# Both heads' scores of a row block issued together, the low key products on 64 rows each, in pairs five to eight

## The chip, the cores and the metric

The kernel runs on one core of a Trainium2 chip. The metric is the device time of one execution in microseconds; the median of three runs of the kernel before is 777.73 us (777.62 to 779.82).

## What is computed

One inference step of a single layer: 512 prompt frames and 64 sample frames (576 columns together) go through a joint projection, two kinds of attention with eight heads of 64 dimensions each, an output projection, an MLP with squared ReLU and a gated embedding. The change touches the scores of the second kind, the sparse attention of the prompt, which picks 128 keys for each query by an indexer's score:

```python
def dsa_attend(q, k, v, iq, ik, iw, q_pos, k_pos, topk):
    logits = jnp.einsum('bqhd,bld->bqhl', iq, ik, preferred_element_type=jnp.float32)
    score = jnp.einsum('bqh,bqhl->bql', iw.astype(jnp.float32), jax.nn.relu(logits))
    ...
    s = jnp.einsum('bqhd,bqkhd->bhqk', q, kg, preferred_element_type=jnp.float32) * HEAD_DIM ** -0.5
    p = jax.nn.softmax(jnp.where(valid[:, None], s, NEG), axis=-1)
    return jnp.einsum('bhqk,bqkhd->bqhd', p.astype(vg.dtype), vg)
```

The kernel doesn't gather keys: it computes all scores of a block and adds a bias that sends the keys not chosen away.

## The kernel before

**Two numbers for one.** A float32 operand is split into a high part that TensorE's F32R type holds and a low remainder, both F32R. A product then takes high by high, low by high and high by low. The projections (`gemm`, line 279) do this with three matmuls of 288 columns for each 128 rows of depth.

**Pairs of heads.** The sixteen heads go in eight pairs, `p` = 0 to 7; 0 to 3 are the forgetting attention, 4 to 7 (pairs five to eight) the sparse one. A pair's queries and keys stand transposed, 64 dimensions of the even head in rows 0 to 63 and of the odd head in rows 64 to 127. For the even head `qE` holds the high part in rows 0 to 63 and the low part in rows 64 to 127, and `kE` the high part in both halves (the second by a DMA, line 737); for the odd head, `qO` and `kO` have the halves the other way round. So one matmul over 128 rows gives high by high and low by high (line 825). The low part of the keys stands in `KL` (buffers `KLP`): rows 0 to 63 for the even head, rows 64 to 127 for the odd one. In pairs one to four the other half of `KL` carries two rows of the forget gate against a row of ones in `Q2`; in pairs five to eight it is zero, and the second matmul (line 827) multiplies 64 rows of keys and 64 rows of zeros.

**Jobs and ticks.** A pair has nine jobs: row blocks `i` = 0 to 3 of 128 queries, each for the even and then the odd head, with (i+1)·128 keys, and one job for the sample frames. Each tick takes one new job, in three micro-steps (`PLAN`, line 917): the first has `addmax` (DVE: scores plus bias, with the row's extreme, line 835) of the job before and `exp` (ACT) of the one before that; the second `ptrans` (transposes on TensorE, tile `T`) of the fourth before; the third `qk` of the new job, `pevac` (copies `T` out of PSUM; DVE in pairs five to eight, line 878) and `pv` (weights times values, line 898). `drive` puts 27 such micro-steps between the 24 pieces of six matmuls of the next pair's projection (`proj`), so TensorE's order is: six projection matmuls, one micro-step, and so on. During pairs five to seven these are the projections of pairs six to eight, during pair eight those of the output projection.

**The ring.** Scores `S`, transposes `T` and the tiles `X` (token-major values in `v_out`, sample outputs in `pv`) take turns in three PSUM banks (tag "R", line 296). A new tile starts once the tile that had its bank has been read: `S` by `addmax`, `T` by `pevac`, `X` by a copy on ACT. Two more facts matter: until pair five DVE also chooses the keys of the sparse attention (lines 642 and 644), and `v_out` of the pair before writes its two `X` tiles in the first two ticks of a pair.

Of the kernel before, what the change touches and what calls it, by code (L numbers as in the profile page):

```python
# [36 lines left out]
def tile_hybrid_step(ctx: ExitStack, tc: tile.TileContext, I, O):  # L37
    nc = tc.nc
    PE, ACT, DVE, POOL, SP = nc.tensor, nc.scalar, nc.vector, nc.gpsimd, nc.sync
# [255 lines left out]
    def psum_1(tag, bufs, dt=F32):  # L295
        return psA.tile([128, 512], dt, name=tag, tag="V" if tag == "V" else "R", bufs=1 if tag == "V" else 3)
# [505 lines left out]
    Q2 = cT = None  # L802
# [9 lines left out]

    def qk(j):
        P = pair[j["p"]]
        ps = psum_1("S", 1)
        if j["s"]:
            g, pp = divmod(j["p"], 4)
            PE.matmul(ps[:, :PAST + NS], QB[j["p"] % 2], KcT[g][:, pp], start=True, stop=True)
            j["S"] = ps[:, :PAST + NS]
        else:  # L820
            i, hh = j["i"], j["hh"]
            n = (i + 1) * 128
            c = slice(i * 128, i * 128 + 128)
            Q, K = P["q" + "EO"[hh]], P["k" + "EO"[hh]]
            PE.matmul(ps[:, :n], Q[:, c], K[:, :n], start=True, stop=False)  # L825
            Q = P["Q2"][:, hh] if j["p"] < 4 else Q
            PE.matmul(ps[:, :n], Q[:, c], P["KL"][:, hh, :n], start=False, stop=True)  # L827
            j["S"] = ps[:, :n]

    def addmax(j):  # L830
        n = j["S"].shape[1]
# [80 lines left out]

    def jobs_of(p):
        out = [dict(p=p, hh=hh, i=i, s=False, close=i % 2 == 1 and hh == 1) for i in range(4) for hh in range(2)]
        return out + [dict(p=p, s=True, close=True)]

    PLAN = (((oevac, 6), (addmax, 1), (exp, 2), (make_bias, 0), (make_bias, -1)),
            ((ptrans, 4), (norm, 2)),
            ((qk, 0), (pevac, 4), (pv, 5)))

    all_jobs = [j for p in range(8) for j in jobs_of(p)]
    tick_no = [0]

# [614 lines left out]
```

## Time and profile before

| | |
|---|---|
| median of three runs | 777.73 us |
| the profiled execution | 777.55 us, of which its span is 775.8 us |
| TensorE busy (matmuls / weight loads) | 765.7 / 749.7 us |
| DVE / ACT / POOL busy | 563.3 / 459.0 / 119.5 us |
| granted TensorE clock | 1.00 throughout |

Rows of the timeline read: start in us from the span's start, duration in us, engine, line of the kernel, operation, output tile and inputs, rows by columns of weights, partitions by elements of the moving operand, count of instructions merged in the row, and in brackets the idle time ahead of it with what ended it. PE are matmuls, PEld are weight loads, which overlap them. A matmul's duration is that from its start to its last result, and successive ones overlap, so what a matmul costs is read from one start to the next.

### The profile page before, as it was taken

Reading aid. Unit: us, or ns where it says so; the run is one execution under the profiler, and the core shown is the slowest. Engines: PE = TensorE matmul, PEld = TensorE weight load, DVE = VectorE, ACT = ScalarE, POOL = GpSimd, SP = SyncE. Lnnn points to the kernel's source line nnn. Section 1 sums busy time; section 2 is a strip of 40 time slices with the busy share of each in tenths; the row PEclk is TensorE's granted clock in tenths of the full one; section 3 lists DMA queues with packets and bytes.
Section 4 is the critical chain, followed back from the end, with each engine's and each line's share of the span. In section 5 each row is a group of like instructions: output and inputs, shape, how many; then the busy total and the mean of one; then the engine's idle time right before and its main releaser. Section 6 shows DMA issues by size and latency. Waiting matters only on the chain.

```text
span 775.8 us, 14798 instructions
## 1 busy us (share of the span) xinstructions
PE 765.7 (99%) x5766; PEld 749.7 (97%) x5766; DVE 563.3 (73%) x1196; ACT 459.0 (59%) x963; POOL 119.5 (15%) x122
## 2 busy tenths in 40 slices
PE   8999999999999999999999999999999999999997
PEld 8989999999999999999999999999999999999997
DVE  7679888897557566899988766767667776657553
ACT  5468777899988644685365443445434455526351
POOL 8117535343421000300000000000000000022100
PEclk9999999999999999999999999999999999999999
DMA  8636334362313225321242322332222314630001
GB/s 304 201 43 148 123 103 117 95 196 85 97 57 104 77 82 185 137 99 56 82 136 87 104 80 60 107 109 82 82 82 82 109 56 124 231 121 29 28 29 68
DMA packets 31126, 81.43 MB, mean 105 GB/s; under 512 B 5072, under 2 KB 10192, under 8 KB 30928
## 3 DMA queue, kind: packets, MB, share of 16 engines
q1 hardware_dynamic: 30768, 80.27, 33.1%
q8 instruction: 45, 0.74, 0.4%
q10 hardware_dynamic: 288, 0.22, 0.1%
q14 instruction: 25, 0.20, 0.1%
HBM read 66.38 MB, written 9.54 MB: 98 GB/s over the span
## 4 chain that ended last, share of the span: by engine, by line
PE 89%; DVE 6%; ACT 2%; issue 1%; DMA 1%; POOL 0%; SPq 0%; DVEq 0%; ACTq 0%
PE g L279 54%; PE m L279 20%; PE n L279 3%; PE V L898 2%; PE T L65 2%; PE S L827 1%; PE S L825 1%; DVE dbias L618 1%; PE m L419 1%; PE m L426 1%; PE S L426 1%; ACT whl L183 1%; PE X L65 1%; DVE whl L187 1%; DVE Y L1203 1%
## 5 line engine op out<-in xcount | busy, mean ns | idle before, releaser
L183 ACT CAST whl<-wraw 128x512 fp32r<-128x512 f32 (+1 forms) x228 | 137.6, 611 | 172.9 <-PE g L279 150.3
L187 DVE TENSOR_TENSOR whl<-wraw,whl 128x512 fp32r<-128x512 f32 (+1 forms) x194 | 132.0, 692 | 69.6 <-ACT whl L183 69.3
L279 PE MATMUL m<-AH,whl 128*128 128x288 f32 x736 | 177.8, 308 | 0.0
L279 PE MATMUL g<-BH,whl 128*128 128x288 f32 (+2 forms) x784 | 162.5, 296 | 0.0
L279 PEld LDWEIGHTS m<-AH,whl 128*128 128x128 f32 x736 | 126.5, 188 | 1.9 <-issue 1.0
L279 PEld LDWEIGHTS g<-BH,whl 128*128 128x128 f32 x784 | 127.7, 188 | 0.3
L279 PE MATMUL g<-BL,whl 128*128 128x288 f32 (+2 forms) x392 | 115.3, 295 | 0.0
L279 PE MATMUL m<-AL,whl 128*128 128x288 f32 x368 | 109.1, 296 | 0.0
L279 PE MATMUL g<-hidO,whl 128*128 128x288 f32 (+2 forms) x768 | 103.8, 295 | 0.0
L279 PE MATMUL g<-hidE,whl 128*128 128x288 f32 (+2 forms) x768 | 103.7, 295 | 0.0
L279 PEld LDWEIGHTS g<-hidO,whl 128*128 128x128 f32 x768 | 102.5, 188 | 0.0
L279 PEld LDWEIGHTS g<-hidE,whl 128*128 128x128 f32 x768 | 102.2, 188 | 0.1
L279 PEld LDWEIGHTS g<-BL,whl 128*128 128x128 f32 x392 | 73.7, 188 | 0.1
L1093 POOL TENSOR_TENSOR ln_s<-Y 128x576 f32<-128x576 f32 (+2 forms) x3 | 4.6, 1519 | 435.2 <-DVE Y L1370 361.9
L279 PE MATMUL g<-s,whl 128*128 128x288 f32 x504 | 71.2, 295 | 0.0
L279 PEld LDWEIGHTS m<-AL,whl 128*128 128x128 f32 x368 | 69.5, 189 | 0.7
L279 PEld LDWEIGHTS g<-s,whl 128*128 128x128 f32 x504 | 68.2, 188 | 0.0
L187 POOL TENSOR_TENSOR whl<-wraw,whl 128x512 fp32r<-128x512 f32 x34 | 44.7, 1314 | 73.6 <-ACT whl L183 49.7
L839 ACT ACTIVATE sP<-sP,st 128x128 f32<-128x128 f32 (+4 forms) x72 | 39.5, 550 | 14.2 <-DVE st L835 13.8
L279 PE MATMUL m<-BH,whl 128*128 128x288 f32 x192 | 43.6, 304 | 0.0
L1346 DVE TENSOR_TENSOR Y<-Y,g 128x576 f32<-128x576 f32 x40 | 29.9, 748 | 14.5 <-PE g L279 14.5
L845 ACT ACTIVATE sP<-sP,st 128x128 f32<-128x128 f32 (+4 forms) x63 | 34.2, 549 | 5.1 <-DVE st L843 4.3
(276 smaller groups left out, 1296.2 us busy)
## 6 DMA issues: line engine op xcount, KB each, us to landing
wraw<-in_w_up_dram SPq DMA_DIRECT2D x32, 512.0 KB, 3.5
wraw<-in_w_down_dram SPq DMA_DIRECT2D x32, 512.0 KB, 3.5
wraw<-in_w_qkv_dram SPq DMA_DIRECT2D x23, 512.0 KB, 3.6
wraw<-in_w_gate_dram SPq DMA_DIRECT2D x8, 512.0 KB, 4.1
wraw<-in_w_o_dram SPq DMA_DIRECT2D x8, 384.0 KB, 3.1
out_vT_dram<-v SPq DMA_DIRECT2D x8, 288.0 KB, 2.1
Y<-in_xT_dram SPq DMA_DIRECT2D x8, 288.0 KB, 4.7
PLD<-PL SPq DMA_DIRECT2D x4, 576.0 KB, 3.0
```

The source lines that it names most:

```text
L65: PE.transpose(out, in_, ident[:n, :n])
L183: ACT.copy(self.hv[h][0], src)
L187: eng.tensor_tensor(lv, src, f(hv), OP.subtract)
L279: PE.matmul(ps, W(w, kw, wc), a[:, ka, cols], start=(first and i == 0), stop=(last and i == n - 1))
L419: PE.matmul(mk[:, h, :HW], w0(part, k), a[:, k, h * HW:(h + 1) * HW], start=(k == 0 and i == 0), stop=(k == 7 and i == 2))
L426: PE.matmul(acc[b][:n[b], :304], a[:, k, b * 128:b * 128 + n[b]], ixw(part, k), start=(k == 0 and i == 0), stop=(k == 7 and i == 2))
L618: DVE.scalar_tensor_tensor(dst[:n, :nk], r[:n, :nk], w, dst[:n, :nk], op0=OP.mult, op1=OP.add)
L825: PE.matmul(ps[:, :n], Q[:, c], K[:, :n], start=True, stop=False)
L839: ACT.activation(j["P"], j["P"], AF.Exp, bias=j["st"][:, 0:1], scale=-1.0, accum_out=j["st"][:, 2:3])
L845: ACT.mul(j["P"], j["P"], j["st"][:, 3:4])
L898: PE.matmul(P["O"][r, (i - 1) * 128 + c.start:(i + 1) * 128], P["vt"][:, kb, r], t[:, hh, kb, c], start=(kb == 0), stop=(kb == i))
L1346: later(0, lambda y=y, m=m: DVE.tensor_tensor(y, y, m[:, :, :HW], OP.add))
```

## The change

In pairs five to eight `qk` of the even head's job issues the scores of both heads of the row block, and `qk` of the odd head's job does nothing. First come the two products over 128 rows, then the two products with the low keys, now over 64 rows each: rows 0 to 63 for the even head, rows 64 to 127 for the odd one, which leaves the zeros out. The two `S` tiles are taken from the ring together. Pairs one to four issue what they issued, and `addmax` and all later stages keep their ticks.

```diff
     def qk(j):
         P = pair[j["p"]]
-        ps = psum_1("S", 1)
         if j["s"]:
+            ps = psum_1("S", 1)
             g, pp = divmod(j["p"], 4)
             PE.matmul(ps[:, :PAST + NS], QB[j["p"] % 2], KcT[g][:, pp], start=True, stop=True)
             j["S"] = ps[:, :PAST + NS]
-        else:
-            i, hh = j["i"], j["hh"]
-            n = (i + 1) * 128
-            c = slice(i * 128, i * 128 + 128)
-            Q, K = P["q" + "EO"[hh]], P["k" + "EO"[hh]]
-            PE.matmul(ps[:, :n], Q[:, c], K[:, :n], start=True, stop=False)
-            Q = P["Q2"][:, hh] if j["p"] < 4 else Q
-            PE.matmul(ps[:, :n], Q[:, c], P["KL"][:, hh, :n], start=False, stop=True)
-            j["S"] = ps[:, :n]
+            return
+        if j["p"] >= 4 and j["hh"]:
+            return
+        i = j["i"]
+        n = (i + 1) * 128
+        c = slice(i * 128, i * 128 + 128)
+        both = [j] if j["p"] < 4 else [j, j["mate"]]
+        for x in both:
+            x["S"] = psum_1("S", 1)[:, :n]
+            PE.matmul(x["S"], P["q" + "EO"[x["hh"]]][:, c], P["k" + "EO"[x["hh"]]][:, :n], start=True, stop=False)
+        for x in both:
+            hh = x["hh"]
+            if j["p"] < 4:
+                PE.matmul(x["S"], P["Q2"][:, hh, c], P["KL"][:, hh, :n], start=False, stop=True)
+            else:
+                r = slice(hh * 64, hh * 64 + 64)
+                PE.matmul(x["S"], P["q" + "EO"[hh]][r, c], P["KL"][r, hh, :n], start=False, stop=True)
...
     def jobs_of(p):
         out = [dict(p=p, hh=hh, i=i, s=False, close=i % 2 == 1 and hh == 1) for i in range(4) for hh in range(2)]
+        for a, b in zip(out[::2], out[1::2]):
+            a["mate"] = b
```

Two places on TensorE show what it moves; the numbers behind the names tell one tile from the next, and the brackets name the engines and DMA queues that an instruction waits for. The first is the first row block of pair five. Before, the even head's two products stand ahead of a piece of the projection and the first `X` tile, and the odd head's two products two pieces later:

```order
L825 MATMUL S_2425<-kE_2116,qE_2267 128x128 [waits DMAHW4_49,DVE_49,Activation_49]
L827 MATMUL S_2425<-KLP0_149,qE_2267 128x128 [waits Pool_49]
L279 MATMUL m_2395<-AH_58,whl_2149 128x288
L279 MATMUL m_2395<-AL_59,whl_2149 128x288
L279 MATMUL m_2395<-AH_58,whl_2149 128x288 x2
L279 MATMUL m_2395<-AL_59,whl_2149 128x288
L279 MATMUL m_2395<-AH_58,whl_2149 128x288
L65 MATMUL X_2436<-ident_60,v32_2393 128x128 [waits DVE_49,Activation_49]
```

With the change:

```order
L829 MATMUL S_2425<-kE_2116,qE_2267 128x128 [waits DMAHW4_49,DVE_49,Activation_49]
L836 MATMUL S_2425<-KLP0_149,qE_2267 128x128 [waits Pool_49]
L829 MATMUL S_2427<-kO_2117,qO_2268 128x128 [waits DMAHW5_49,DVE_49]
L836 MATMUL S_2427<-KLP0_149,qO_2268 128x128 [waits Pool_49]
L279 MATMUL m_2395<-AH_58,whl_2149 128x288
L279 MATMUL m_2395<-AL_59,whl_2149 128x288
L279 MATMUL m_2395<-AH_58,whl_2149 128x288 x2
L279 MATMUL m_2395<-AL_59,whl_2149 128x288
L279 MATMUL m_2395<-AH_58,whl_2149 128x288
L65 MATMUL X_2439<-ident_60,v32_2393 128x128 [waits Activation_49]
```

The odd head's score tile now takes the bank that `X` took, and with it the wait for DVE; and in this one block the two 64-row products (L836) don't stand side by side, because the odd head's product over 128 rows stands between them. The second place is the third row block of pair five, which stands for the other fifteen. Before, the even head's two products and the sample output `X` behind them:

```order
L825 MATMUL S_2617<-kE_2116,qE_2267 128x384 [waits DVE_49]
L827 MATMUL S_2617<-KLP0_149,qE_2267 128x384
L887 MATMUL X_2622<-PTs_2561,Vc_139 128x128 [waits Activation_49]
L888 MATMUL X_2622<-PTs_2561,VS1_158 128x128
L279 MATMUL m_2523<-AH_58,whl_2278 128x288
```

With the change:

```order
L829 MATMUL S_2617<-kE_2116,qE_2267 128x384 [waits DVE_49]
L829 MATMUL S_2619<-kO_2117,qO_2268 128x384 [waits Activation_49]
L836 MATMUL S_2617<-KLP0_149,qE_2267 128x384
L836 MATMUL S_2619<-KLP0_149,qO_2268 128x384
L895 MATMUL X_2625<-PTs_2561,Vc_139 128x128 [waits DVE_49]
L896 MATMUL X_2625<-PTs_2561,VS1_158 128x128
L279 MATMUL m_2526<-AH_58,whl_2278 128x288
```

Here the four products stand in a row, the two over 64 rows next to each other, and `X` waits for DVE where it waited for ACT.

## Prediction

> **What bounds the kernel now.** I read the page first, for the engine that carries the span, then the busy times by stage, then TensorE's timeline around the scores of pairs five to eight. The page's busy times and its chain of waits:
>
> ```profile
> PE 765.7 (99%) x5766; PEld 749.7 (97%) x5766; DVE 563.3 (73%) x1196; ACT 459.0 (59%) x963; POOL 119.5 (15%) x122
> PE 89%; DVE 6%; ACT 2%; issue 1%; DMA 1%; POOL 0%; SPq 0%; DVEq 0%; ACTq 0%
> ```
>
> TensorE carries the chain. By stage (start:end, length, then busy us of PE, PEld, DVE, ACT, POOL, the clock, DMA), with a row for each of pairs five to eight:
>
> ```profile
> 162.00:191.00 29.00, 27.97 (x218) 26.75 (x217) 23.30 (x75) 26.29 (x60) 10.93 (x10) 1.00 0.51 167
> 191.00:219.00 28.00, 28.00 (x219) 26.69 (x218) 16.97 (x51) 25.36 (x60) 10.51 (x9) 1.00 0.29 86
> 219.00:247.00 28.00, 28.00 (x219) 26.94 (x218) 17.33 (x51) 23.50 (x56) 5.19 (x4) 1.00 0.31 96
> 247.00:281.00 34.00, 33.69 (x262) 32.35 (x261) 22.23 (x62) 22.57 (x55) 0.00 (x0) 1.00 0.26 75
> ```
>
> The reader is to see that TensorE is idle only 1.0 us in pair five and 0.3 us in pair eight. So whatever TensorE saves or loses here reaches the end one for one, unless it goes into those waits.
>
> **What the low products cost before.** A block's cost is read from the start of its first product to the start of the projection matmul behind it: for 128 keys (to the second matmul behind, since the first one there starts late), then 384 and 512 keys.
>
> ```profile
> 171.62 0.22 PE L825 MATMUL S<-kO,qO 128*128 128x128 f32 x1
> ...
> 171.98 0.29 PE L279 MATMUL m<-AL,whl 128*128 128x288 f32 x1
> ...
> 185.39 0.34 PE L825 MATMUL S<-kO,qO 128*128 128x384 f32 x1
> 185.74 0.29 PE L279 MATMUL m<-AH,whl 128*128 128x288 f32 x1
> ...
> 190.61 0.39 PE L825 MATMUL S<-kO,qO 128*128 128x512 f32 x1
> 191.07 0.30 PE L279 MATMUL m<-AH,whl 128*128 128x288 f32 x1
> ```
>
> The pace of the projection, twelve matmuls of 288 columns in 1.60 us, is 0.133 us each or 0.46 ns a column:
>
> ```profile
> 219.35 1.60 PE m L279 x12
> ```
>
> So two products cost 0.36 - 0.13 = 0.23 us with 128 keys, 0.35 with 384 and 0.46 with 512. The latter two are the pace of the columns (2 x 384 x 0.46 ns = 0.35), which gives 0.24 with 256 keys; with 128 keys it is 0.11 a product where columns alone take 0.06, so there the load of 128 columns of weights, 0.11 us, sets the cost. All four products of a block: 0.46, 0.47, 0.70, 0.93; a pair 2.56, the four pairs 10.2 us. The low halves are 5.1 us. If two 64-row products ran beside each other at no other cost, half of that, 2.5 us, would go.
>
> **What a change of the array's shape costs.** No product of two 64-row halves stands in this trace, but two relatives do. The output products (L898) put two heads beside each other on 64 columns each, and the second norm has one product over 64 rows. First all L898 products (shortest, median and longest duration in ns, starts, shapes), then the matmuls around one group of them, then the matmuls and the weight loads around the 64-row product:
>
> ```profile
> L898 PE MATMUL V<-PT,vtok x192: 272/379/431, 92.2 to 295.6; 128*64 128x256 f32 x128, 128*64 128x128 f32 x64
> 176.95 0.28 PE L827 MATMUL S<-KLP,qO 128*128 128x256 f32 x1
> 177.16 0.44 PE L898 MATMUL V<-PT,vtok 128*64 128x256 f32 x2
> ...
> 179.47 0.40 PE L279 MATMUL m<-AH,whl 128*128 128x288 f32 x1
> 179.72 0.30 PE L279 MATMUL m<-AL,whl 128*128 128x288 f32 x1
> ...
> 737.58 0.47 PE L65 MATMUL n<-ident,ln_r 128*128 128x128 f32 x2
> 737.98 0.39 PE L279 MATMUL g<-BH,whl 128*128 128x256 f32 x1
> 738.20 0.28 PE L279 MATMUL g<-BL,whl 128*128 128x256 f32 x1
> ...
> 737.78 0.13 PEld L65 LDWEIGHTS n<-ident,ln_r 64*128 64x128 f32 x1 [0.17 <-issue]
> 737.97 0.19 PEld L279 LDWEIGHTS g<-BH,whl 128*128 128x128 f32 x1
> 738.08 0.19 PEld L279 LDWEIGHTS g<-BL,whl 128*128 128x128 f32 x1
> ```
>
> Two things are seen. First, the pair does run side by side: two L898 products together last 0.44 us in the record where one of their kind lasts 0.43 at most. Second, each passage between shapes empties the array. Ahead of L898 the full product takes 0.21 us instead of the 0.12 its 256 columns need: 0.09 lost. The weight load of the 64-row product is not fetched ahead as all others are; its queue stands still for 0.17 us first. Behind it the next full load comes 0.19 later, after the array has emptied again, and the first full matmul (737.98 to 738.20) takes 0.22 instead of 0.12, because its own load, 0.11 us, now lies bare. Behind L898 the same is 0.25 instead of 0.13.
>
> The Trainium skill says this of the array in "TensorEngine Tiling (Array Packing)", Key Properties: a change of the tiling mode, as against a change of the tile, drains TensorE. The trace agrees, with the 0.09 and 0.11 us above. The skill also speaks for the change: "TensorE: Matmul & The Clock Gate", in its part on packing small matmuls, gives a pack as one product's time plus about 4 ns a tile, with no term for switching; by that alone 2.5 us would be saved, as in the first rival.
>
> **The sum for a block.** For one visit to the 64-row shape I take: emptying 0.09, the bare load of the low products' weights 0.11, emptying again 0.09, the bare load of the next full matmul 0.11, together 0.40 us. The load of 0.11 is the price of these very 128 columns in the 128-key row above; the low end is the whole 64-row visit of the second norm, 0.09 + 0.19 + 0.10 less some 0.04 for its own columns, 0.34. A block then costs the even and the odd product over 128 rows, 0.40, and one low product's columns for both heads:
>
> 128 keys: 0.11 + 0.06 + 0.40 + 0.06 = 0.63 against 0.46, +0.17.
> 256 keys: 0.12 + 0.12 + 0.40 + 0.12 = 0.76 against 0.47, +0.29.
> 384 keys: 3 x 0.176 + 0.40 = 0.93 against 0.70, +0.23.
> 512 keys: 3 x 0.235 + 0.40 = 1.10 against 0.93, +0.17.
>
> That is +0.86 a pair and +3.4 us for four pairs: at every size the saved product is worth less than the two changes of shape. The low end of 0.34 takes 16 x 0.06 = 1.0 us off.
>
> **The ring.** The first block of pair five is different. There the profile has the one long wait of TensorE in these stages: X waits until DVE has read the sample scores of pair four (matmuls, then DVE's rows).
>
> ```profile
> 167.80 0.29 PE L279 MATMUL m<-AH,whl 128*128 128x288 f32 x1
> 169.12 0.30 PE L65 MATMUL X<-ident,v 128*128 128x128 f32 x1 [1.03 <-DVE st L835]
> ...
> 168.02 0.70 DVE L642 MAX8 st<-dbias 128x8 f32<-128x512 f32 x1
> 168.63 0.34 DVE L835 CUSTOM_DVE_ANT_0 sP<-S,biasS 128x192 f32<-128x192 f32 x1
> ```
>
> DVE is held by the choice of keys (L642), which the change leaves ahead of that read. With the change the odd head's score tile takes this bank, and it stands six projection matmuls earlier. TensorE reaches it at about 167.2 and still waits until about 169.1; the even head's visit to the 64-row shape vanishes in that wait. After it come the odd head's own visit (0.06 + 0.40 + 0.06 = 0.52), the six matmuls that used to run before the wait (0.80) and only then X: 1.3 us later than 169.12. At 171.62 the odd head's 0.23 is gone. So this block costs +1.1 instead of +0.17, that is +0.9 more. What waited behind X on TensorE are the projection and all stages after it; nothing there waits long enough to give it back.
>
> Elsewhere a second score tile is held a tick longer, so a `T` must now be copied out before X of the third block. In pair five that copy and X stand like this:
>
> ```profile
> 182.43 0.38 PE L887 MATMUL X<-PTs,Vc 128*128 128x128 f32 x2
> ...
> 182.90 0.27 DVE L878 COPY PT<-T 128x128 f32<-128x128 f32 x1
> ```
>
> The copy ends at 183.17, 0.74 after X used to start. With the change X stands behind the odd head's products and the visit, which is 0.93 - 0.35 = 0.58 later. DVE's work follows TensorE's delay in part. I take 0 here, and up to 0.6 as the upper end. `addmax`, `exp` and what follows keep their ticks: the scores come up to half a microsecond later inside a tick of about 3 us. The operands of the odd head are wanted a tick earlier, and the even head already waits for nearly the same instructions.
>
> Sum: +3.4 + 0.9 = +4.3 us. The span goes from 775.8 to 780.1, the profiled execution from 777.55 to 781.85. It stands 0.18 below the median, so I forecast **782.0 us**, +0.55%.
>
> **The rivals.**
>
> *The change of shape is hidden (not slower).* If the 64-row products and their loads slip between the full ones, 2.5 us go and the ring's 0.9 stays: 776.1 us. It decides once a visit costs less than (2.5 - 0.9) / 16 = 0.10 us. For it speaks that L898's pairs run side by side; against it the 0.17 us of the load queue ahead of a 64-row product. Chance 0.06.
>
> *Cheap visits.* 0.34 a visit and the ring's wait half absorbed: 782.0 - 1.0 - 0.5 = 780.5, and somewhat less if an emptying falls into another wait. Chance 0.12.
>
> *The halves don't run beside each other.* Then each block pays a second load or a second product, whichever is longer: 0.11 + 0.12 + 0.18 + 0.23 = 0.64 a pair, 2.6 us in all: 784.6. Nothing in this trace shows two row halves together, only two column halves. Chance 0.13.
>
> *The ring holds more.* If the copy ahead of X comes 0.6 late in the third block of every pair, that is 2.4 us: 784.4. Against it: DVE is at 17 of 28 us in pairs six and seven, where no keys are chosen any more. Chance 0.10.
>
> **How the numbers follow.** The forecast keeps 0.59, with 780.9 to 783.4 as its own spread. The range takes in the cheap visits and the two dearer cases, 779.8 to 784.7, and leaves the hidden case and the tails out. A measurement of this kernel tells about 0.3% from no change, so within 0.3% means 775.4 to 780.1: most of the hidden case and the lower part of the cheap one, 0.12; faster 0.03; slower 0.85.
>
> **What would show it.** In the profile after, each block should show the two 64-row loads with an idle stretch ahead of them, and the first full matmul behind them about 0.1 us late; a 512-key block should take about 1.1 us from its first product to the next projection matmul. The two low products of a block should start within hundredths of a microsecond of each other; starts 0.1 to 0.2 apart would mean the third rival. TensorE's wait in pair five should stand ahead of the odd head's first product, near 169.1, at about 1.5 to 2 us. Loads fetched ahead of the 64-row products, or DVE's read of the sample scores coming earlier, would make the forecast wrong.

## The result, and the profile after

The changed kernel takes 783.9 us (median of six runs, 782.39 to 785.4) where the kernel before took 778.42 us in the same comparison (six runs, 777.61 to 779.82). The ratio is 1.0072, with a 95% interval of 1.0061 to 1.0083: slower by 0.7%. The profiled execution took 782.39 us with a span of 780.7 us, 4.84 us above the span before (782.39 - 777.55). The other five runs were longer by 1.5 us, one of them by 3.0, at a mean clock of 0.997 where the profiled one has 0.999. The kernel before has such runs too, three of its six here (779.11 to 779.82, against 777.61 to 777.73), so the change costs 4.8 us between the longer runs too (779.1 and 783.9). The last experiment and the last section come back to the 1.5 us.

The page's busy times and its chain of waits, after:

```profile
PE 769.3 (99%) x5766; PEld 748.1 (96%) x5766; DVE 564.4 (72%) x1196; ACT 457.9 (59%) x963; POOL 118.5 (15%) x122
PE 88%; DVE 6%; ACT 3%; issue 1%; DMA 1%; POOL 0%; SPq 0%; DVEq 0%; ACTq 0%
```

TensorE bounds as before and is busy 3.6 us longer with the same 5766 matmuls. Here are the stages of pairs five to eight, with the same columns as before; each row ends at the same projection matmul as its counterpart there:

```profile
162.06:192.80 30.74, 29.08 (x218) 26.49 (x217) 24.34 (x79) 27.66 (x63) 11.16 (x10) 1.00 0.49 158
192.80:221.41 28.61, 28.61 (x218) 26.25 (x217) 15.73 (x47) 24.51 (x58) 10.34 (x8) 1.00 0.28 83
221.41:250.25 28.84, 28.84 (x220) 26.48 (x219) 17.00 (x49) 23.39 (x55) 5.19 (x4) 1.00 0.29 85
250.25:285.82 35.57, 34.74 (x262) 31.99 (x262) 23.41 (x64) 21.34 (x55) 0.00 (x0) 1.00 0.26 78
```

The rows are 1.74, 0.61, 0.84 and 1.57 us longer than 29, 28, 28 and 34. That is 4.76 of the 4.84 us, so the loss arises in these four pairs and nothing behind them gives it back. In pairs six and seven TensorE is busy from end to end: what grew there is its own work. In pairs five and eight it is idle 1.66 and 0.83 us, where it was idle 1.0 and 0.3.

**One block of 512 keys.** TensorE's matmuls around the last block of pair five, then the weight loads of the same stretch:

```profile
189.18 0.39 PE L829 MATMUL S<-kE,qE 128*128 128x512 f32 x1
189.41 0.40 PE L829 MATMUL S<-kO,qO 128*128 128x512 f32 x1
189.73 0.50 PE L836 MATMUL S<-KLP,qE 64*128 64x512 f32 x1
189.74 0.50 PE L836 MATMUL S<-KLP,qO 64*128 64x512 f32 x1
190.16 0.40 PE L279 MATMUL m<-AH,whl 128*128 128x288 f32 x1
190.40 0.30 PE L279 MATMUL m<-AL,whl 128*128 128x288 f32 x1
...
189.18 0.19 PEld L829 LDWEIGHTS S<-kO,qO 128*128 128x128 f32 x1
189.73 0.18 PEld L836 LDWEIGHTS S<-KLP,qE 64*128 64x128 f32 x1 [0.36 <-issue]
189.73 0.18 PEld L836 LDWEIGHTS S<-KLP,qO 64*128 64x128 f32 x1
190.16 0.19 PEld L279 LDWEIGHTS m<-AH,whl 128*128 128x128 f32 x1 [0.24 <-issue]
```

The two low products start 0.01 us apart by these rows (3 ns in the trace's own resolution). They do run side by side: from 189.73 to 190.16 both pass in 0.43 us, one product's 0.23 for the columns and 0.20 that belong to the change of shape. The other half of the price stands on either side. The second full product holds the array for 0.32 us (189.41 to 189.73) where its columns need 0.23, and the first projection matmul takes 0.24 (190.16 to 190.40) instead of 0.133. The loads show why: neither the 64-row loads nor the first full load behind them is fetched ahead. Both stand with an idle stretch in front of them. The 64-row loads of the blocks with 256 to 512 keys carry no wait for a semaphore in the trace, so no other engine holds them back.

Read this way for each size, from a block's first product to the projection's resumed pace, in us for both heads:

| keys | before | after | forecast after | difference measured |
|---|---|---|---|---|
| 128 (pairs six and seven) | 0.45 | 0.63 | 0.63 | +0.18 |
| 256 | 0.476 | 0.749 | 0.76 | +0.27 |
| 384 | 0.70 | 0.925 | 0.93 | +0.225 |
| 512 | 0.92 | 1.09 | 1.10 | +0.17 |

Behind the 384 keys stands `X`, also a full product; its columns are taken off. Two blocks of 128 keys and four of each other size make 0.36 + 1.08 + 0.90 + 0.68 = 3.0 us.

**The first block of pair five**, TensorE's matmuls and the read that it waits for on DVE:

```profile
166.97 0.22 PE L829 MATMUL S<-kE,qE 128*128 128x128 f32 x1
167.13 0.32 PE L836 MATMUL S<-KLP,qE 64*128 64x128 f32 x1
169.11 0.33 PE L829 MATMUL S<-kO,qO 128*128 128x128 f32 x1 [1.66 <-DVE st L843]
169.37 0.33 PE L836 MATMUL S<-KLP,qO 64*128 64x128 f32 x1
169.62 0.40 PE L279 MATMUL m<-AH,whl 128*128 128x288 f32 x1
...
173.13 0.29 PE L279 MATMUL m<-AL,whl 128*128 128x288 f32 x1
...
168.71 0.34 DVE L843 CUSTOM_DVE_ANT_0 sP<-S,biasS 128x192 f32<-128x192 f32 x1
```

The wait that stood ahead of `X` now stands ahead of the odd head's first product and ends at the same time, 169.11. The odd head's visit and the six projection matmuls follow it. The projection matmul that stood at 171.98, behind the odd head's old place, is at 173.13; 0.06 of that is an offset of the whole trace, and 1.09 us are lost.

**Pair eight** has what the forecast did not. TensorE's wait ahead of the first `X`, the two products of its first block, and then two rows of ACT:

```profile
254.82 0.29 PE L279 MATMUL m<-BH,whl 128*128 128x288 f32 x1
255.57 0.65 PE L65 MATMUL X<-ident,v 128*128 128x128 f32 x4 [0.45 <-ACT v L685]
...
257.18 0.22 PE L829 MATMUL S<-kE,qE 128*128 128x128 f32 x1
257.78 0.33 PE L829 MATMUL S<-kO,qO 128*128 128x128 f32 x1 [0.38 <-ACT vtok L770]
...
256.53 0.73 ACT L853 ACTIVATE sP<-sP,st 128x512 f32<-128x512 f32 x1
257.15 0.57 ACT L770 COPY vtok<-X 128x512 f32<-128x512 f32 x1
```

The odd head's score tile takes the bank in which `X` was written at 255.57. ACT copies that `X` out only at 257.15, behind the exponentials of the pair before, until 257.72; the odd head's product starts at 257.78. Before, one tile fewer had been taken from the ring at this point, and the even head's products passed without a wait. This block costs 1.22 us instead of 0.45, and the wait ahead of `X` is 0.14 longer than before.

All of TensorE's waits on a tile in these stages (tile, releaser, us in total, count, longest):

```profile
PE S L829 <- DVE st L843: 1.7, 1, 1.7
PE X L65 <- ACT v L685: 0.5, 1, 0.5
PE S L829 <- ACT vtok L770: 0.4, 1, 0.4
```

The account of the span: 3.0 for fourteen blocks, 1.1 for pair five's first, 0.78 for pair eight's first and 0.14 for its `X`, less 0.2 for a gap behind pair six's first odd block that closes. Together 4.8, as measured.

### The profile page after: what moved, and what is told of

It is laid out like the page before. It is cut to its first block, busy times and chain, and to the rows that moved or that the text cites. A ratio compares the mean times of both kernels' runs of the same rounds, so it can differ in the third digit from the quotient of the medians.

```text
span 780.7 us, 14800 instructions
## 1 busy us (share of the span) xinstructions
PE 769.3 (99%) x5766; PEld 748.1 (96%) x5766; DVE 564.4 (72%) x1196; ACT 457.9 (59%) x963; POOL 118.5 (15%) x122
## 4 chain that ended last, share of the span: by engine, by line
PE 88%; DVE 6%; ACT 3%; issue 1%; DMA 1%; POOL 0%; SPq 0%; DVEq 0%; ACTq 0%
PE g L279 54%; PE m L279 19%; PE n L279 3%; PE V L906 2%; PE T L65 2%; DVE dbias L618 1%; PE S L829 1%; PE m L419 1%; ACT whl L183 1%; PE m L426 1%; PE S L426 1%; DVE whl L187 1%; PE S L836 1%; DVE Y L1213 1%; PE S L833 1%
```

## The experiments

Three questions were open: whether the loss is the change of shape or the order, what the ring's share is, and where the 1.5 us of the longer executions come from. All kernels below compute the whole of the reference. Ratios are against the kernel before in the same comparison.

**together_128_rows**: the order of the change, the shape of before.

```diff
-                r = slice(hh * 64, hh * 64 + 64)
-                PE.matmul(x["S"], P["q" + "EO"[hh]][r, c], P["KL"][r, hh, :n], start=False, stop=True)
+                PE.matmul(x["S"], P["q" + "EO"[hh]][:, c], P["KL"][:, hh, :n], start=False, stop=True)
```

> Both heads' scores issued together as in the change, but the low products over 128 rows with the zeros, as before: no change of the array's shape. Theory (each visit to the 64-row shape costs 0.40 us, and the order alone costs only the ring's waits): a block takes what it took before (0.45, 0.47, 0.70, 0.92 us), TensorE still waits about 1.7 us for DVE in pair five's first block and about 0.5 us for ACT in pair eight's; span 776.9 to 777.4, some 3.5 us under the change. Rival (issuing the heads together, with two score tiles held in the ring, is what costs): span 779.5 or more, within 1 us of the change.

Measured: 781.06 us (779.68 to 781.08), ratio 1.0036 (1.0022 to 1.0049). Three of its four runs have a span of 779.3, the shortest one 777.9. The blocks cost what they cost before (0.45 to 0.92 us), so the 2.1 us from 775.8 to 777.9 are the order alone, and the 2.8 us from there to 780.7 the shape. The order costs more than expected, 777.9 where 777.4 was the upper end. The waits on tiles in its profiled execution (one of the three at 779.3) show by what:

```profile
PE S L829 <- DVE st L842: 1.8, 1, 1.8
PE X L65 <- ACT v L685: 0.9, 1, 0.9
PE S L829 <- ACT vtok L770: 0.4, 1, 0.4
```

Besides pair five's wait there are 1.3 us for ACT in pair eight, where there were 0.3 before.

**apart_64_rows**: the shape of the change, the order of before.

```diff
+            r = slice(0, 128) if j["p"] < 4 else slice(hh * 64, hh * 64 + 64)
             Q = P["Q2"][:, hh] if j["p"] < 4 else Q
-            PE.matmul(ps[:, :n], Q[:, c], P["KL"][:, hh, :n], start=False, stop=True)
+            PE.matmul(ps[:, :n], Q[r, c], P["KL"][r, hh, :n], start=False, stop=True)
```

> The heads issued in their own ticks as before, but each low product over its 64 rows: 32 visits to the 64-row shape in place of 16, none shared. Theory: a visit costs 0.34 us more than the two products cost before with 128 keys and about 0.39 with 256 to 512, so 2 x 4 x (0.34 + 3 x 0.39) = 12.1 us, less some 0.3 that falls into the wait in pair five: span 787 to 788. Rival (the order and the ring are what costs, not the shape): span 776 to 777.

Measured: 787.45 us (787.0 to 787.54), ratio 1.0121 (1.0107 to 1.0135), span 785.8. So 32 visits without anything saved cost 10.0 us. That is below the forecast by over a microsecond, and the timeline says where. Two of its visits, the even head's with 512 keys and the odd head's with 256:

```profile
189.27 0.39 PE L825 MATMUL S<-kE,qE 128*128 128x512 f32 x1
189.59 0.50 PE L828 MATMUL S<-KLP,qE 64*128 64x512 f32 x1
190.01 0.40 PE L279 MATMUL m<-AH,whl 128*128 128x288 f32 x1
190.25 0.29 PE L279 MATMUL m<-AL,whl 128*128 128x288 f32 x1
...
177.59 0.28 PE L825 MATMUL S<-kO,qO 128*128 128x256 f32 x1
177.79 0.38 PE L828 MATMUL S<-KLP,qO 64*128 64x256 f32 x1
178.11 1.95 PE L899 MATMUL V<-PT,vtok 128*64 128x256 f32 x18
```

With 512 keys the head costs 0.98 (189.27 to 190.25) less the projection's 0.133, or 0.85 us, +0.39 against before, and it is +0.39 with 384 keys and with 256. Where the 64-column products of `pv` follow at once, the way back to the full shape falls away: 0.52 us from the head's first product to `pv` (177.59 to 178.11), against 0.33 before, +0.20 from the unrounded 0.522 and 0.326. With 128 keys a head costs 0.51, which is 0.12 for its columns and 0.39, against 0.225 before; that already held 0.10 of waiting for loads, so it is +0.285. Eight heads at 0.285, four at 0.20 and twenty at 0.39 make 10.9; TensorE's waits give back the rest, mainly that ahead of pair eight's `X`, which is gone (0.5). The price of a visit holds; the sum had missed the two exceptions and this gain.

**first_blocks_as_before** and **pair_five_first_as_before**: the change, with the first block of all four pairs, or of pair five alone, issued and shaped as before. The diff is that of the first; the second has `pack = j["p"] > 4 or j["p"] == 4 and j["i"] > 0`.

```diff
-        if j["p"] >= 4 and j["hh"]:
+        pack = j["p"] >= 4 and j["i"] > 0
+        if pack and j["hh"]:
             return
...
-        both = [j] if j["p"] < 4 else [j, j["mate"]]
+        both = [j, j["mate"]] if pack else [j]
...
+            elif not pack:
+                PE.matmul(x["S"], P["q" + "EO"[hh]][:, c], P["KL"][:, hh, :n], start=False, stop=True)
```

> The change without the first row block (128 keys) of each pair, which is issued as before. Theory: twelve packed blocks at +0.28, +0.23 and +0.17 us, four times 0.68 = 2.7 us, no new wait of the ring: TensorE's wait in pair five is back at X with 1.0 us; span 778.3 to 778.7. Rival (the cost is spread evenly over the blocks): three quarters of the 4.9 us, span 779.5.

> The change, but the first row block of pair five alone is issued as before, each head in its tick over 128 rows. Theory (that block costs 1.1 us by the ring's wait for DVE, and the wait of 2 us is what lowers the clock in most executions): span 779.4 to 779.8 where the clock holds, and the share of executions that are 1.5 us longer falls from five in six to about that of the kernel before, one in four; median 781.2 to 781.5. Rival (the clock falls for another reason, the drains for one): most executions still 1.5 us longer, median 782.8 or more.

Measured: 780.95 us (780.19 to 781.73), ratio 1.0042 (1.0027 to 1.0057), span 778.5; and 783.11 us (781.65 to 783.15), ratio 1.0064 (1.005 to 1.0078), span 779.9. From 780.7, leaving out pair five's first block gives back 0.8 us, and leaving out the other three 1.4 more. Matmul by matmul, pair five's block is worth 1.07 us, as in the account above. But TensorE, now earlier, loses 0.11 of it ahead of the third block's `X` (in both kernels), and 0.27 in pair six in the second kernel, whose first block there has the odd head's product 0.29 us behind the even one's (196.85 and 197.14) where the change has 0.06. The first kernel doesn't meet that wait: its 1.4 us are these 0.27, the 0.36 of pairs six and seven from the table, and 0.77 of pair eight. What is left, 2.7 us above 775.8, is the twelve blocks of 256 to 512 keys, 0.27 + 0.225 + 0.17 four times. Three of five runs of the second kernel were still 1.5 us longer than the other two, and two of four of the first. With the median of 783.11 the rival's condition (782.8 or more) is met, and the forecast share of one in four is missed: pair five's long wait can't be the only source of the longer runs, few as these are.

**before_later_X**: the kernel before, with the two `X` tiles of pair five's projection two pieces later, so that the long wait has no tile to stand at.

```diff
-                side = delayed(2, v_out(p - 1))
+                side = delayed(4 if p == 5 else 2, v_out(p - 1))
```

> The kernel before, with the token-major values of pair five written two pieces of the projection (twelve matmuls, 1.6 us) later, in the first two ticks of pair five alone, so that their X tile no longer waits for DVE's read of the sample scores. Theory (that 1.0 us is a wait of the ring that reaches the end one for one): TensorE's wait falls to 0.2 us or less, span 774.8 to 775.1, 0.8 to 1.0 us under the kernel before. Rival (the wait moves to the next tile of the ring, or a later wait takes it): span 775.6 to 776.

Measured: 777.51 us against 777.56, ratio 1.0 (0.9991 to 1.0009), span 775.7. The 1.0 us was not to be had in this way, as the rival said. The waits on tiles of this kernel:

```profile
PE T L65 <- ACT PT L876: 0.4, 1, 0.4
PE X L65 <- ACT v L685: 0.3, 1, 0.3
PE T L65 <- DVE st L835: 0.3, 1, 0.3
```

`T` now waits for the same read of DVE (0.3) and for ACT (0.4). With three banks, another tile stands at the wait.

**before_X_in_V, change_X_in_V and together_X_in_V**: `X` of `v_out` is taken out of the ring and put into the bank of the output products (tag "V"), one micro-step later in pair eight. The first is this edit to the kernel before. The second is the same edit to pair_five_first_as_before. The third is the second with all low products over 128 rows.

```diff
     def tok_out(src):
-        m = psum_1("X", 1)
+        m = psum_1("V", 1)
...
     def tok_out_s(src):
-        m = psum_1("X", 1)
+        m = psum_1("V", 1)
...
-        side = delayed(1, v_out(7))
+        side = delayed(2, v_out(7))
```

> The kernel before, with the token-major values written into the PSUM bank of the output products (tag V), which is free in the first ticks of a pair, and out of the ring; in pair eight they also come one piece of the projection later. Theory (TensorE's 1.0 us for DVE in pair five and 0.3 to 0.5 us for ACT in pair eight are waits of the ring and of the values' copy, and reach the end): waits of at most 0.3 us each remain, span 774.6 to 775.1. Rival (DVE is late in pair five whatever stands in the ring, so the wait moves to the next transposes, as it did when X came later): span 775.4 to 775.8.

> The change with its waits of the ring taken away: pair five's first block as before, the token-major values in the bank of tag V, one piece of the projection later in pair eight. What is left is the 64-row shape in fifteen blocks. Theory: three blocks at +0.18, four each at +0.27, +0.23 and +0.17 us, 3.2 us over the kernel before with the same banks (span 774.6): span 777.6 to 778.0. Rival (with the waits gone some of the switching is hidden, or new waits take the place): span under 777 or over 778.5.

> The same, but the low products over 128 rows with the zeros: the heads are issued together in fifteen blocks and the shape never changes. Theory (without the ring's waits the order costs nothing): span 774.4 to 774.9, that of the kernel before with the same banks. Rival (a score tile held a tick longer still stalls TensorE): span 775.5 or more.

| kernel | median, us | before, us | ratio (95%) | span, us |
|---|---|---|---|---|
| before_X_in_V | 776.36 | 777.58 | 0.9982 (0.9974 to 0.9991) | 774.6 |
| change_X_in_V | 779.67 | 777.6 | 1.0026 (1.0017 to 1.0036) | 777.9 |
| together_X_in_V | 777.16 | 777.6 | 0.9996 (0.9987 to 1.0005) | 775.4 |

The waits on tiles, of before_X_in_V in the first row and of together_X_in_V in the three behind it:

```profile
PE S L825 <- ACT sP L845: 0.2, 1, 0.2
```

```profile
PE X L898 <- DVE PT L889: 0.4, 1, 0.4
PE T L65 <- ACT PT L887: 0.3, 1, 0.3
PE S L830 <- ACT sP L856: 0.3, 1, 0.3
```

With the ring relieved, the kernel before gets 0.18% faster, and its waits shrink from 1.3 to 0.2 us. In the same surroundings the 64-row shape costs 777.9 - 775.4 = 2.5 us. The pairing itself, with both heads in full shape, still holds 0.8 us (774.6 to 775.4) in three short waits, which the expectation had at 0.3 at most and its rival at 0.9 or more; the rows fit a ring that is a little too small in several places once a second score tile is held for a tick. The two costs don't simply add: change_X_in_V stands 3.3 us above before_X_in_V, which is nearly all the 3.2 of its fifteen blocks by the table, so with the 64-row shape hardly any of the 0.8 shows. So even without the ring's long waits the halves side by side are no gain, and the quickest of all these kernels is before_X_in_V, without the change.

**change_again**: the changed kernel once more, for the place of the 1.5 us.

> The change once more, with a profile, to see where the clock falls in the executions that last 783.9 us in place of 782.4. Theory (TensorE's 2 us of idleness in pair five's first block lowers the granted clock): if this execution is one of the longer ones, the clock is at half for a stretch of about 3.4 us that begins within 4 us of 169, and the span is 782.2. Rival (the clock falls elsewhere, as it may in the kernel before): the stretch lies elsewhere.

Measured: 784.12 us, span 782.4, one run. The stages from 165 us on, in short stretches, of change_again and then of the profiled execution of the changed kernel above (one row; columns as before, the clock is the third number from the end):

```profile
165.00:170.00 5.00, 3.34 (x24) 2.97 (x23) 4.80 (x13) 4.94 (x13) 1.60 (x2) 1.00 0.95 312
170.00:172.00 2.00, 2.00 (x11) 1.98 (x10) 2.00 (x8) 0.93 (x4) 0.96 (x1) 0.50 0.84 283
172.00:174.00 2.00, 2.00 (x13) 2.00 (x12) 1.73 (x6) 1.23 (x3) 0.00 (x0) 0.66 0.82 293
174.00:176.00 2.00, 2.00 (x18) 2.00 (x17) 0.82 (x3) 1.65 (x5) 0.00 (x0) 1.00 0.27 106
```

```profile
170.00:172.00 2.00, 2.00 (x19) 2.00 (x18) 2.00 (x9) 1.63 (x6) 0.85 (x1) 1.00 0.94 286
```

Half the clock is granted from 169.96 us for 3.41 us, as the trace's own record of the clock has it, 0.7 us behind the end of pair five's wait: 11 matmuls in two microseconds instead of 19. The profiled execution with 780.7 us has no such stretch, and the two spans differ by 1.7 us.

## Why the prediction was right, and what it missed

The forecast was 782.0 us, with a range of 779.8 to 784.7. The median is 783.9, and the sign and the range hold. By its steps:

- *TensorE bounds, and what it loses reaches the end.* Right: 4.76 us lost in pairs five to eight are 4.84 at the end.
- *Two passages between shapes, 0.40 us a visit.* Right, to within 0.02 us at every size, with the parts as named: an emptying and a bare load on each side. apart_64_rows shows it by itself, at 0.39. Fourteen blocks give 3.0 us where the forecast has 3.4 less the first blocks of pairs five and eight, 3.1.
- *The halves run side by side.* Right, 3 ns apart; the rival in which they don't falls, and so does the hidden change of shape. The cheap visit, 0.34, falls by the 0.40 measured. It was also read a little low from the second norm: the starts there in the trace (737.578, 737.779, 737.975, 738.197) and 64 columns of its own, 0.03, give 0.36.
- *The ring in pair five, +1.1 us for its first block.* Right: 1.09, with the wait at 169.11. It was put at 1.5 to 2 us and is 1.66.
- *The other waits of the ring, taken as 0.* Here the sum failed. Where the forecast looked, at the third block's `X`, no wait came. (Where TensorE isn't held by 1.1 us in pair five's first block it does come, in pair five alone: 0.3 us for DVE's copy in change_X_in_V and 0.4 in together_X_in_V.) In pair eight ACT copies `X` out late, and there 0.78 us went where +0.17 was put down, and 0.14 more ahead of `X`. These 0.75 us too much, less the 0.2 of the gap that closed in pair six, are the 0.5 by which the span was missed (4.84 against 4.3). The rival "the ring holds more" had the resource and the wrong place; it had argued from DVE, and it was ACT.
- *The clock taken as full.* Wrong for most executions. The profiled one kept it (782.39, 0.4 from the forecast), the five others did not. In change_again the loss of clock lies right behind pair five's wait, a cost of that wait which the sum had left out. That each of the five lost it at the same place is inferred from length and mean clock; it was seen in change_again alone. So the median lies 1.9 us above the forecast, 1.5 of it by a mechanism that the prediction doesn't have. The range still holds because its upper end was set for two other cases, halves one after the other and a late copy by DVE, and neither came: that much is luck.

The step on shape decided the sign. Sixteen visits at 0.40 us cost 6.4 us, and the product that a block saves is worth 3.0 by the table (0.22, 0.13, 0.175 and 0.23 us by size, four times).

## What to carry to other kernels

Running two halves of the array beside each other pays only where the products between two changes of shape save more than the passages cost: here 0.40 us there and back against 0.46 ns for each column saved, an estimated 870 columns, while a score tile has 512; so products of one shape should be gathered into one run, which no run here tries, or put next to a group that leaves the full shape anyway, where the visit cost half (+0.20). When a change takes two tiles at once from a ring of buffers, ask of every tile that now gets a bank one place earlier which engine has yet to read it. An unrelated tile taken out of that ring, and written one micro-step later in one pair, was worth 1.2 us here by itself.

## What the runs showed of the hardware

**A wait of 1.7 us can cost 1.5 us more behind it, depending on when it falls.** In three profiles the wait of pair five is about the same, and the clock is not:

| kernel | wait of TensorE | full clock since | half clock |
|---|---|---|---|
| the change, first profile | 167.45 to 169.11 | 4.60 | none before 779.4 |
| change_again | 167.58 to 169.24 | 6.12 | 169.96 to 173.37 |
| together_128_rows | 167.27 to 169.07 | 6.82 | 170.66 to 174.07 |

The half clock lasts 3.413 us, and it begins 163.84 us after full clock began in both cases, which is 48 times 3.413. If the clock is decided at the end of windows of that length, counted from there, the wait lies whole in one window in the latter two (166.55 to 169.96 and 167.24 to 170.66) and is cut in two at 168.4 in the first.

All eleven profiles on record, two of them of the change, bear this out. Each stretch of full clock lasts a whole number of such windows, from 48 (163.84 us) to 228 (778.24 us in apart_64_rows). And TensorE's idle time, meaning time under no matmul's row, counted in each window so laid out, separates the outcomes without exception:

| TensorE idle in one window | where | clock in the next window |
|---|---|---|
| 0.99 and 0.67 | the change, first profile, its wait cut in two | full |
| 1.04 | first_blocks_as_before, pair five | full |
| 1.47 | before_X_in_V, the first window (the most of any window not listed here is 1.44) | full |
| 1.50 | before, 769.5 to 772.9, behind the last matmul | full |
| 1.66 | change_again, pair five | half |
| 1.80 | together_128_rows, pair five | half |
| 1.90 | apart_64_rows, 779.8 to 783.2, behind the last matmul | half |
| 2.21 to 3.41 | the end of the other ten profiles, the first window there of more than 1.5 | half |

So in these traces the clock falls once TensorE idles somewhere between 1.50 and 1.66 us of one 3.413 us window, about half of it, and the position of the wait decides. No run moved that position on purpose, and the ends of matmuls in a profile are modelled, so the border is known no more closely than this. The Trainium skill, "TensorE: Matmul & The Clock Gate", Part 1, gives a free-running window of 3413 ns, with which the trace agrees; it lets the clock fall after one idle window, and here TensorE was idle for only half of one.

This doesn't explain every run that is 1.5 us longer. The kernel before idles 1.03 us in pair five in its profile and still has four such runs of fifteen, and together_X_in_V, with no wait above 0.4 us in its profile, has three of ten. Some of them show no lost clock at all: one of pair_five_first_as_before has a mean clock of 1.0, and both of change_X_in_V have 0.999, as its quicker ones, where one such stretch at half clock takes 0.002 off the mean. None of these runs left a trace, so a second source stays open.

**Next to another small shape a visit costs half.** Leaving the 64-row shape directly for the 64-column shape costs one passage, +0.20 us instead of +0.39, as apart_64_rows shows with 256 keys.

**A weight load of half the rows lasts as long as a full one.** The record has 0.18 us for 64 rows by 128 columns and 0.19 for 128 by 128, and the two 64-row loads of a pair run at the same time.
